# Split-weight buffers that are 256 bytes longer, with the feature-major halves written 64 bytes in

## Chip, cores and metric

The kernel runs on one core of one Trainium2 chip, as one launch. The metric is the device time of that launch in microseconds; several runs are taken and their median counts. One further execution was profiled, and every time below that is not called a median comes from it.

## What is computed

One layer of a hybrid decoder trunk over 256 tokens of width 2048, in float32. Three token mixers (gated DeltaNet, Mamba-2, GLA) share one input projection, are gated and merged, and two more sub-layers follow. Cut to what matters here:

```python
h = rmsnorm(x, pre_mix_norm[i])
... = jnp.split(h @ w_in[i], split_idx, axis=-1)          # 2048 x 15920
y_dn, y_ssm, y_gla = ...                                  # three mixers, chunked scans
up = jnp.einsum('btnm,nmd->btnd', branches, w_branch[i])  # 3 x (1024 x 2048)
mixed = jnp.sum(gates * up, axis=2) @ w_out[i]            # 2048 x 2048
x = x + rmsnorm(mixed, post_mix_norm[i])
h = rmsnorm(x, pre_mlp_norm[i])
m = jnp.square(jax.nn.relu(h @ w_up[i])) @ w_down[i]      # 2048 x 8192, 8192 x 2048
x = x + rmsnorm(m, post_mlp_norm[i])
ple_gate = jax.nn.sigmoid(rmsnorm(x, ple_pre_norm[i]) @ w_ple_gate[i])
x = x + rmsnorm((p[i] @ w_ple_proj[i]) * ple_gate, ple_post_norm[i])
```

## The kernel before

All large products run on TensorE in the type float32r. To keep float32 accuracy, each operand is split into a rounded half `hi` and the rest `lo`, and a product is three passes: hi times hi, hi times lo, lo times hi. The weights are streamed from memory and split on the way by `weights`: a 512 KB DMA on SyncE's queue brings two k-tiles of up to 512 columns into a tile `raw` (128 partitions by 2 x 512 numbers), ScalarE copies it into `hi` (line 300), and VectorE writes `raw - hi` into `lo` (line 170, the helper `tt`). Each of the three tags has four buffers of 4096 bytes per partition that are used in turn.

Two routines use the pieces. In `gemm_tok` (token-major) a 128x128 block of the activations is the stationary operand, which TensorE loads ahead of the product, and `hi` or `lo` streams through as the moving operand, 512 columns at a time (344 or 352 in some units); the profile names such a product `mm<-hi,ahi`, moving operand first. In `gemm_feat` (feature-major) a 128x128 block of `hi` or `lo` is stationary and the activations stream, 256 columns at a time: `mm<-ahi,hi`, `mm<-ahi,lo`, `mm<-alo,hi`. Both issue through line 114. Feature-major are 27 units of 192 products: 6 for DeltaNet, 3 for Mamba-2, 2 for GLA and 16 for `w_up`; all else is token-major. The order of the work on every engine is the order in which the kernel's text is written, with small pieces of the mixers (`br<-...`) put between the products by `background`.

Where the buffers lie matters for this change. In the built program all partitions have the same layout, and these are byte addresses in a partition. `hi` has its four buffers at 43360, 47456, 51552 and 55648, `lo` at 59744, 63840, 67936 and 72032; the activations `ahi` and `alo` lie at 76128 and 92512; the tiles `m` (squared MLP activations) and the split mixer outputs (profile name `b`) lie in multiples of 2048 bytes behind. All of these start at 352 modulo 512, and all operands of the large products are cut out of them at multiples of 512 bytes, except that 344 and 352 columns end earlier. So in each of the large products the stationary and the moving operand start at the same place modulo 512. A few small products of the GLA mixer do not: `gkh`, `gkl`, `ga` and the tiles with the profile name `c` start at 416 modulo 512, `gtr` at 352, `le16` (profile name `le`) at 32, and the stationary operands of the mixers' own float32 products start at many places: the first of those at 542.63 us in the rows below starts at 96 modulo 512.

Of the kernel before, what the change touches and what calls it, by code (L numbers as in the profile page):

```python
# [10 lines left out]
F32R = mybir.dt.float32r  # L11
# [4 lines left out]
P = 128  # L16
# [36 lines left out]
def tile_hybrid_block(ctx: ExitStack, tc: tile.TileContext, *args):  # L53
# [14 lines left out]
    wp = ctx.enter_context(tc.tile_pool(name="wp", bufs=4))  # L68
# [6 lines left out]
    def nm(p):  # L75
        cnt[0] += 1
        return f"{p}{cnt[0]}"
# [22 lines left out]
    def mbank(n=512):  # L100
        return ps.tile([P, n], F32, tag="mm", bufs=4, name=nm("mm_"))

    def r3(ap, b):
        return ap.rearrange("p (a b) -> p a b", b=b)
# [45 lines left out]
    def background(limit=2.6):  # L150
        end = clk[0] + limit
        go = True
        while go and clk[0] < end:
            go = False
            for t in list(tasks):
                if t.done or t.ready > clk[0] or t.blocked():
                    continue
                t.step()
                go = True
                if clk[0] >= end:  # L160
                    break
# [7 lines left out]
    def tt(eng, o, i0, i1, op):  # L169
        eng.tensor_tensor(out=o, in0=i0, in1=i1, op=op)  # L170
# [111 lines left out]
    CK = 2  # L282
# [1 line left out]

    urgent = [False]

    def weights(parts, k0, ck):

        n = sum(p[2] for p in parts)
        raw = wp.tile([P, CK, 512], F32, tag="raw", bufs=4, name=nm("raw"))[:, :ck, :]  # L290
        hi = wp.tile([P, CK, 512], F32R, tag="hi", bufs=4, name=nm("hi"))[:, :ck, :]
        lo = wp.tile([P, CK, 512], F32R, tag="lo", bufs=4, name=nm("lo"))[:, :ck, :]
        with (tc.high_priority(AHEAD) if urgent[0] else ExitStack()):
            o = 0
            for w, c, m in parts:
                nc.sync.dma_start(
                    out=raw[:, :, o:o + m],
                    in_=w[k0 * P:(k0 + ck) * P, c:c + m].rearrange("(k p) n -> p k n", p=P))
                o += m
            A.copy(out=hi[:, :, :n], in_=raw[:, :, :n])  # L300
            tt(V, lo[:, :, :n], raw[:, :, :n], hi[:, :, :n].bitcast(F32), ALU.subtract)
        return hi, lo

    def gemm_tok(parts, act, nkt, evac, k0=0, held=1):


        n = sum(p[2] for p in parts)
        pb = [mbank() for _ in range(NT)]
        steps = []
        for kc in range(0, nkt, CK):  # L310
            hl = weights(parts, k0 + kc, CK)
            steps += [(kc, k, t, hl) for k in range(CK) for t in range(NT)]
            if kc + CK == nkt:
                steps.sort(key=lambda p: p[2])
            elif kc + CK > nkt - held * CK:
                continue
            for i, (kc_, k, t, (hi, lo)) in enumerate(steps):
                kt = kc_ + k
                xh, xl = act(kt, t)
                o = pb[t][:, :n]  # L320
                PE.matmul(o, lhsT=xh, rhs=hi[:, k, :n], start=(kt == 0), stop=False)
                PE.matmul(o, lhsT=xh, rhs=lo[:, k, :n], start=False, stop=False)
                PE.matmul(o, lhsT=xl, rhs=hi[:, k, :n], start=False, stop=(kt == nkt - 1))
                if i % 2:
                    background()
                if kt == nkt - 1:
                    with tc.high_priority():
                        evac(t, pb[t][:, :n])
            steps = []

    def gemm_feat(parts, act, nkt, evac):

        n = sum(p[2] for p in parts)
        nb = n // 256
        pb = [mbank() for _ in range(nb)]
        for kc in range(0, nkt, CK):
            hi, lo = weights(parts, kc, CK)
            steps = [(k, c) for k in range(CK) for c in range(n // P)]
            if kc + CK == nkt:
                steps.sort(key=lambda p: p[1] // 2)  # L340
            for i, (k, c) in enumerate(steps):
                kt = kc + k
                xh, xl = act(kt, None)
                o = pb[c // 2][:, (c % 2) * S:(c % 2 + 1) * S]
                wh, wl = hi[:, k, c * P:(c + 1) * P], lo[:, k, c * P:(c + 1) * P]
                PE.matmul(o, lhsT=wh, rhs=xh, start=(kt == 0 and c % 2 == 0), stop=False,
                          skip_group_check=True)
                PE.matmul(o, lhsT=wl, rhs=xh, start=False, stop=False, skip_group_check=True)
                PE.matmul(o, lhsT=wh, rhs=xl, start=False, stop=(kt == nkt - 1), skip_group_check=True)
                if i % 4 == 3:  # L350
                    background()
        with tc.high_priority():
            for b in range(nb):
                evac(b, r3(pb[b], S))
# [77 lines left out]
    def feat_conv(cw, nch, ncol, c0, bias, c_w, act=hact):  # L432

        nct = ncol // P
        xp = t4()
        xp3 = r3(xp, 260)
        V.memset(xp3[:, :nct, 0:4], 0.0)

        def evac(b, pb):
            tt(V, xp3[:, 2 * b:2 * b + 2, 4:260], pb, r0bc.unsqueeze(1).broadcast_to([P, 2, S]), ALU.mult)  # L440

        gemm_feat([(w_in, c0, ncol)], act, KT, evac)
        cw, bias = cw(), bias and bias()
        y = t4()
        for c in range(nct):
            yc = y[:, c * S:(c + 1) * S]
            ch = c_w + c

            def wj(j):
                return cw[:, j * nch + ch:j * nch + ch + 1]  # L450
            if bias is None:
                A.activation(out=yc, in_=xp3[:, c, 4:260], func=AF.Copy, scale=wj(3))
            else:
                A.activation(out=yc, in_=xp3[:, c, 4:260], func=AF.Identity, scale=wj(3), bias=bias[:, ch:ch + 1])
            for j in (2, 1, 0):
                stt(yc, xp3[:, c, 1 + j:257 + j], wj(j), yc, ALU.mult, ALU.add)
        A.activation(out=y[:, :nct * S], in_=y[:, :nct * S], func=AF.Silu)
        return y
# [104 lines left out]
    def first_params():  # L563
        urgent[0] = True
        load_params()
        return prm["cw0"]
    dn_q0 = feat_conv(first_params, 24, 512, C_DNQ, None, 0, act=hact0)
    gemm_tok([(w_in, C_DNB, 352)], hact, KT, mk(0))
    dn_alog, dn_dtb, ss_alog, ss_dtb, ss_d, gainT, dcwT, scwT = (
        prm[k] for k in ("dn_alog", "dn_dtb", "ss_alog", "ss_dtb", "ss_d", "gains", "cw0", "cw1"))  # L570
# [20 lines left out]
    for c0, n in ((352, 344), (696, 344)):  # L591
        gemm_tok([(w_in, C_DNB + c0, n)], hact, KT, mk(c0))
# [174 lines left out]
    ss_dtr = const.tile([P, NT, 16], F32, name="ss_dtr")  # L767
    mk = tok_cols(16, ss_dtr, ss_y3)
    gemm_tok([(w_in, C_SDT, 16), (w_in, C_SZ, 336)], hact, KT, mk(0))
    dt = const.tile([P, NT, 16], F32, name="dt")  # L770
    adt = const.tile([P, NT, 16], F32, name="adt")
# [125 lines left out]
    def feat_plain(c0, scale):  # L897
        y = t4()

        def evac(b, pb):  # L900
            stt(r3(y[:, :1024], S)[:, 2 * b:2 * b + 2, :], pb, scale,
                r0bc.unsqueeze(1).broadcast_to([P, 2, S]), ALU.mult, ALU.mult)

        gemm_feat([(w_in, c0, 512)], hact, KT, evac)
        return y
# [101 lines left out]
    def y_tiles():  # L1007
        hi = t8().bitcast(F32R)[:, :2048]
        lo = t8().bitcast(F32R)[:, :2048]
        return r3(hi, S), r3(lo, S)  # L1010
# [21 lines left out]
    for b in range(2):  # L1032
# [8 lines left out]
        hi, lo = y_tiles()  # L1041
# [8 lines left out]
    hi, lo = y_tiles()  # L1050
# [80 lines left out]
    for cb in range(4):  # L1131
        def evac(t, pb, cb=cb):
            if cb == 0 and t == 0:
                phase_b()
            if t == 0:
                mg.append([tb("mx") for _ in range(NT)])
            if cb == 0:
                A.sqrt(out=sm(1), in_=r0[:, :1])
            square_sum(pb, 512, ssp[:, t, cb:cb + 1])
            tt(V, mg[cb][t], pb, gains["g1"][:, cb * 512:(cb + 1) * 512], ALU.mult)  # L1140
# [131 lines left out]
```

## Time and profile before

| | |
|---|---|
| median of 3 runs | 1887.17 us (1881.85 to 1887.25) |
| profiled execution, its own time | 1882.98 us |
| its span, first to last instruction | 1881.2 us |
| TensorE busy | 1846.9 us, 98% |
| VectorE busy | 1161.0 us, 62% |
| ScalarE busy | 934.9 us, 50% |
| mean granted clock of TensorE | 0.993 of full speed |
| chain that ended last | 69% of the span on TensorE, 67% on line 114 |

[...] What one product costs is the distance from its start to the start of the next one, and that is read from the timeline. [...]

### The profile page before, as it was taken

The page shows a single profiled execution, that of the slowest core. Times are in us where ns is not written, and L with a number is a line of the kernel's source. Part 1 is how long each engine was busy: PE and PEld are TensorE (multiplying, and loading weights), DVE is VectorE, ACT ScalarE, POOL GpSimd, SP SyncE. Part 2 cuts the span into 40 slices and gives each one's busy share as a digit, 9 for nine tenths or more (in the row PEclk, how much of TensorE's full clock was granted, in tenths as well). Part 3 has the DMA queues.
Part 4 walks back from the last instruction along what each step waited for, and adds up shares of the span by engine and source line. Part 5 has one row for each costly group of instructions (what it writes and reads, how often), then busy time and mean ns, then how long its engine had stood idle before and what let it go on. Part 6 is the DMA issues. An engine that isn't in the chain of part 4 may idle for free.

```text
span 1881.2 us, 28343 instructions
## 1 busy us (share of the span) xinstructions
PE 1846.9 (98%) x11256; PEld 1659.0 (88%) x11256; DVE 1161.0 (62%) x1518; ACT 934.9 (50%) x1200; POOL 183.7 (10%) x243
## 2 busy tenths in 40 slices
PE   8999999899999999999999999999999999999997
PEld 8999989899888788888888898899889988998886
DVE  6567947878566666554565755455555555555675
ACT  6745564576455564454444644444433443444664
POOL 0004814800201220000000000000000000000001
PEclk9999989999999999999999999999999999999999
DMA  7765565465665546667676565666566566656563
GB/s 250 218 184 175 147 186 165 137 182 145 196 201 168 172 143 192 195 183 196 186 246 204 175 185 190 191 189 181 191 192 188 180 192 195 184 182 195 183 207 129
DMA packets 185573, 348.07 MB, mean 185 GB/s; under 512 B 14296, under 2 KB 33103, under 8 KB 184544
## 3 DMA queue, kind: packets, MB, share of 16 engines
q1 hardware_dynamic: 182992, 334.69, 58.8%
q0 software_dynamic: 2416, 11.56, 1.8%
q8 instruction: 88, 1.44, 0.3%
q14 instruction: 45, 0.37, 0.1%
q10 hardware_dynamic: 32, 0.01, 0.0%
HBM read 340.41 MB, written 5.80 MB: 184 GB/s over the span
## 4 chain that ended last, share of the span: by engine, by line
PE 69%; ACT 1%; POOL 1%; DVE 1%; issue 0%; DMA 0%; DVEq 0%; ACTq 0%
PE mm L114 67%; PE br L114 1%; PE br L123 1%; POOL b L170 1%; DVE lo L170 0%; ACT hi L300 0%; DMA raw<-in_w_in_dram 0%; DVE b L173 0%; ACT b L946 0%; ACT L1226 0%; ACT b L945 0%; ACT b L1114 0%; ACT L1236 0%; ACT b L1224 0%; DVE s L173 0%
## 5 line engine op out<-in xcount | busy, mean ns | idle before, releaser
L170 DVE TENSOR_TENSOR lo<-raw,hi 128x1024 fp32r<-128x1024 f32 (+2 forms) x644 | 771.7, 1202 | 621.9 <-ACT hi L300 618.5
L300 ACT CAST hi<-raw 128x1024 fp32r<-128x1024 f32 (+2 forms) x644 | 653.6, 1019 | 807.3 <-PE mm L114 702.3
L114 PE MATMUL mm<-ahi,hi 128*128 128x256 f32 x1728 | 492.2, 285 | 0.0
L114 PE MATMUL mm<-ahi,lo 128*128 128x256 f32 x1728 | 490.8, 284 | 0.0
L114 PE MATMUL mm<-alo,hi 128*128 128x256 f32 x1728 | 490.8, 284 | 0.0
L114 PE MATMUL mm<-hi,ahi 128*128 128x512 f32 (+2 forms) x992 | 372.0, 375 | 0.0
L114 PE MATMUL mm<-lo,ahi 128*128 128x512 f32 (+2 forms) x992 | 369.0, 372 | 2.8 <-DVE lo L170 1.6
L114 PE MATMUL mm<-hi,alo 128*128 128x512 f32 (+2 forms) x992 | 367.6, 371 | 0.0
L114 PEld LDWEIGHTS mm<-ahi,hi 128*128 128x128 f32 x1728 | 333.3, 193 | 0.5 <-ACT ahi L180 0.2
L114 PEld LDWEIGHTS mm<-alo,hi 128*128 128x128 f32 x1728 | 332.8, 193 | 0.8 <-issue 0.8
L114 PEld LDWEIGHTS mm<-ahi,lo 128*128 128x128 f32 x1728 | 333.3, 193 | 0.1
L114 PE MATMUL mm<-hi,m 128*128 128x512 f32 x1024 | 316.0, 389 | 0.0
L114 PEld LDWEIGHTS mm<-hi,m 128*128 128x128 f32 x1024 | 192.2, 188 | 39.9
L114 PEld LDWEIGHTS mm<-lo,ahi 128*128 128x128 f32 x992 | 187.2, 189 | 32.3 <-DVE lo L170 4.0
L114 PEld LDWEIGHTS mm<-hi,ahi 128*128 128x128 f32 x992 | 187.1, 189 | 28.0 <-issue 0.2
L114 PEld LDWEIGHTS mm<-hi,alo 128*128 128x128 f32 x992 | 187.1, 189 | 27.5
L114 PE MATMUL mm<-lo,m 128*128 128x512 f32 x512 | 199.2, 389 | 0.0
L114 PE MATMUL mm<-hi,b 128*128 128x512 f32 x416 | 134.1, 393 | 0.7 <-ACT hi L300 0.7
L114 PEld LDWEIGHTS mm<-lo,m 128*128 128x128 f32 x512 | 96.1, 188 | 19.7
L170 POOL TENSOR_TENSOR b<-b 128x128 f32<-128x128 f32 (+16 forms) x118 | 78.4, 679 | 162.0 <-ACT b L939 149.9
L114 PEld LDWEIGHTS mm<-hi,b 128*128 128x128 f32 x416 | 78.1, 188 | 17.0 <-ACT hi L300 1.1
L114 PE MATMUL mm<-lo,b 128*128 128x512 f32 x208 | 81.3, 391 | 0.8 <-DVE lo L170 0.8
(257 smaller groups left out, 1130.0 us busy)
## 6 DMA issues: line engine op xcount, KB each, us to landing
raw<-in_w_in_dram SPq DMA_DIRECT2D x200, 512.0 KB, 4.1
raw<-in_w_up_dram SPq DMA_DIRECT2D x128, 512.0 KB, 3.8
raw<-in_w_down_dram SPq DMA_DIRECT2D x128, 512.0 KB, 3.8
raw<-in_w_branch_dram SPq DMA_DIRECT2D x48, 512.0 KB, 4.6
raw<-in_w_in_dram SPq DMA_DIRECT2D x48, 344.0 KB, 3.5
raw<-in_w_out_dram SPq DMA_DIRECT2D x32, 512.0 KB, 4.8
raw<-in_w_ple_gate_dram SPq DMA_DIRECT2D x32, 512.0 KB, 4.5
raw<-in_w_in_dram SPq DMA_DIRECT2D x16, 352.0 KB, 3.4
```

The lines of the kernel that those rows point to most:

```text
L114: nc.tensor.matmul(o, lhsT=lhsT, rhs=rhs, start=start, stop=stop, **kw)
L123: nc.tensor.transpose(o, i, ident)
L170: eng.tensor_tensor(out=o, in0=i0, in1=i1, op=op)
L300: A.copy(out=hi[:, :, :n], in_=raw[:, :, :n])
```

## The change

`weights` takes a new argument `off`. The buffers of `hi` and `lo` are made 64 numbers (256 bytes) longer, and the 2 x 512 numbers of a split are placed `off` numbers into the buffer: 0 where the caller is `gemm_tok`, 16 (64 bytes) where it is `gemm_feat`. `raw` is as before.

```diff
+    OFF_TOK, OFF_FEAT = 0, 16
+
-    def weights(parts, k0, ck):
+    def weights(parts, k0, ck, off):
 
         n = sum(p[2] for p in parts)
         raw = wp.tile([P, CK, 512], F32, tag="raw", bufs=4, name=nm("raw"))[:, :ck, :]
-        hi = wp.tile([P, CK, 512], F32R, tag="hi", bufs=4, name=nm("hi"))[:, :ck, :]
-        lo = wp.tile([P, CK, 512], F32R, tag="lo", bufs=4, name=nm("lo"))[:, :ck, :]
+        hi, lo = (r3(wp.tile([P, CK * 512 + 64], F32R, tag=z, bufs=4, name=nm(z))[:, off:off + CK * 512], 512)[:, :ck, :]
+                  for z in ("hi", "lo"))
...
-            hl = weights(parts, k0 + kc, CK)
+            hl = weights(parts, k0 + kc, CK, OFF_TOK)
...
-            hi, lo = weights(parts, kc, CK)
+            hi, lo = weights(parts, kc, CK, OFF_FEAT)
```

The built program has the same instructions in the same order on every engine, with the same waits; only line numbers and addresses differ. `hi` now starts at 43360, 47712, 52064 and 56416 and `lo` at 60768, 65120, 69472 and 73824, that is at 352 modulo 512 in the first and third buffer and at 96 in the second and fourth. `ahi` and `alo` move by 2048 bytes to 78176 and 94560, and so does everything behind them, which leaves their place modulo 512 as it was. In feature-major products the stationary operand therefore starts 64 bytes (first and third buffer) or 320 bytes (second and fourth) behind the moving one, modulo 512, and 64 behind modulo 256 in each of them. In token-major products the moving operand starts where the stationary one does, or 256 bytes from it.

## Rows read from the trace of the kernel before

**Rows 1.** The page, part 4: the chain that ended last, by engine.

```profile
PE 69%; ACT 1%; POOL 1%; DVE 1%; issue 0%; DMA 0%; DVEq 0%; ACTq 0%
```

**Rows 2.** Waits of TensorE: us in total, times, longest; the one for split weights.

```profile
PE mm L114 <- DVE lo L170: 2.4, 3, 0.9
```

**Rows 3.** Groups of products by form, TensorE.

```profile
line engine op names shapes xcount | busy us, mean ns | idle before us <-releasers
L114 PE MATMUL mm<-ahi,hi 128*128 128x256 f32 x1728 | 492.2, 285 | 0.0
...
L114 PE MATMUL mm<-hi,m 128*128 128x512 f32 x1024 | 316.0, 389 | 0.0
L114 PE MATMUL mm<-hi,ahi 128*128 128x512 f32 x704 | 276.5, 393 | 0.0
...
L114 PE MATMUL mm<-hi,b 128*128 128x512 f32 x416 | 134.1, 393 | 0.7 <-ACT hi L300 0.7
```

**Rows 4.** Timeline (start us, duration us, what), TensorE, feature-major, full clock.

```profile
1299.79 0.28 PE L114 MATMUL mm<-ahi,lo 128*128 128x256 f32 x1
...
1300.87 0.28 PE L114 MATMUL mm<-ahi,lo 128*128 128x256 f32 x1
```

**Rows 5.** Timeline of TensorE, token-major, 512 columns.

```profile
1199.63 0.39 PE L114 MATMUL mm<-lo,m 128*128 128x512 f32 x1
...
1200.99 0.39 PE L114 MATMUL mm<-lo,m 128*128 128x512 f32 x1
```

**Rows 6.** A stretch of 3.3 us: busy time of each engine, granted clock.

```profile
core 0: us, PE busy (x) PEld busy (x) DVE busy (x) ACT busy (x) POOL busy (x), PEclk, DMA share, GB/s
300.20:303.50 3.30, 3.30 (x16) 3.30 (x17) 3.30 (x8) 0.00 (x0) 1.27 (x2) 0.50 0.33 101
```

**Rows 7.** Timeline of TensorE in that stretch, feature-major.

```profile
302.09 0.41 PE L114 MATMUL mm<-ahi,lo 128*128 128x256 f32 x1
...
303.15 0.41 PE L114 MATMUL mm<-ahi,hi 128*128 128x256 f32 x1
```

**Rows 8.** Timeline of weight loads around the products that read le16.

```profile
504.13 0.19 PEld L114 LDWEIGHTS mm<-hi,ahi 128*128 128x128 f32 x1
...
504.81 0.19 PEld L114 LDWEIGHTS br<-le,gkh 128*128 128x128 f32 x1
505.04 0.19 PEld L114 LDWEIGHTS br<-le,gkl 128*128 128x128 f32 x1
...
505.37 0.19 PEld L114 LDWEIGHTS mm<-hi,ahi 128*128 128x128 f32 x1
```

**Rows 9.** Timeline of TensorE, the product that runs while ga is loaded.

```profile
556.92 0.39 PE L114 MATMUL mm<-hi,b 128*128 128x512 f32 x1
557.14 0.59 PE L114 MATMUL br<-b,ga 128*128 128x256 f32 x2
```

**Rows 10.** Timeline of TensorE, feature-major product while a float32 operand is loaded.

```profile
359.28 0.28 PE L114 MATMUL mm<-alo,hi 128*128 128x256 f32 x1
359.40 0.66 PE L114 MATMUL br<-c,c 128*128 128x64 f32 x5
```

**Rows 11.** Timeline of TensorE, the product of gkh that runs while gtr is loaded.

```profile
486.42 0.40 PE L114 MATMUL br<-gkh,gtr 128*128 128x512 f32 x1
486.66 0.39 PE L114 MATMUL br<-gkl,gtr 128*128 128x512 f32 x1
```

**Rows 12.** Timeline of TensorE, token-major product while weights 256 bytes apart are loaded.

```profile
542.40 0.39 PE L114 MATMUL mm<-hi,alo 128*128 128x512 f32 x1
542.63 0.49 PE L114 MATMUL br<-b,b 128*128 128x128 f32 x3
```

**Rows 13.** The page, part 5: the two instructions that write lo and hi.

```profile
L170 DVE TENSOR_TENSOR lo<-raw,hi 128x1024 fp32r<-128x1024 f32 (+2 forms) x644 | 771.7, 1202 | 621.9 <-ACT hi L300 618.5
L300 ACT CAST hi<-raw 128x1024 fp32r<-128x1024 f32 (+2 forms) x644 | 653.6, 1019 | 807.3 <-PE mm L114 702.3
```

## The prediction

> **What bounds the kernel now.** I read the chain of waits first. 69% of the span hang on TensorE, and no other engine reaches 2% [rows 1]. The waits say the same from the other side: for split weights TensorE waited 2.4 us in total [rows 2]. DMA, ScalarE and VectorE bring the weights in time, so only what changes the pace of TensorE, or makes one of those three late, can change the time.
>
> The pace is read from the timeline, as the distance between starts; the durations in the groups overlap. In the feature-major stage 9 products take 1300.87 - 1299.79 = 1.08 us, so one comes every 120 ns [rows 4]. In the token-major stage 6 products of 512 columns take 1200.99 - 1199.63 = 1.36 us, 226.7 ns each [rows 5]. The two differ by 256 columns and 106.7 ns, or 0.417 ns a column, one period of 2.4 GHz. 256 columns alone would take 106.7 ns and 512 would take 213.3: each product costs **13.3 ns more than its columns**, at either length. Where the granted clock was 0.50, the lower level of 1.2 GHz [rows 6], 5 products of 256 columns took 303.15 - 302.09 = 1.06 us, 212 ns each [rows 7], which is 256 columns at that clock with nothing over. So the 13.3 ns appear only when the moving operand streams at full rate beside the load of the next weights. The load starts with the product ahead of it: their starts, too, are 0.68 / 3 = 227 ns apart where products of 512 columns run [rows 8].
>
> The stakes follow from the counts. There are 3 x 1728 = 5184 feature-major products [rows 3], which take 5184 x 120 ns = 622 us, a third of the span. **One nanosecond per product is 5.2 us, 0.28% of the time.**
>
> **The change part by part.** *Instructions.* None is added, removed or moved, and no wait either: 0 us. Only durations can change.
>
> *Pace of the feature-major products.* This is the one large term. The change sets the stationary operand 64 bytes further in than the moving one (320 in half of the buffers); before, they agree modulo 512. Only if the 13.3 ns come from two reads that meet at places that depend on this distance can the pace move. The large products show no other distance, and yet within the same 512 bytes they show many: their operands lie at all multiples of 512 bytes from each other, and the pace is 120 ns throughout. For other distances I go to the few small products. While a `gkh` block is loaded, 64 bytes further in than the moving `hi`, just as the change has it, a product of 512 columns takes 505.04 - 504.81 = 0.23 us [rows 8], against 0.227 otherwise. While `ga` is loaded, at the same distance, it is 557.14 - 556.92 = 0.22 us [rows 9]; there are four such in the trace, all 0.22 or 0.23. A feature-major product during which a float32 operand is loaded at that distance takes 359.40 - 359.28 = 0.12 us [rows 10]. All within the 0.01 us of the view. That argues for **no change**, and I take 0 ns, since these rows have the very distance that the change makes.
>
> The bounds come from further away. Upwards: with `gtr` loaded 64 bytes short of the moving `gkh`, the product takes 486.66 - 486.42 = 0.24 us [rows 11], 0.013 more than 0.227, and its duration is 0.40 where the others have 0.39; I read +10 ns. It is a single product, and the distance has the other sign. 5184 x 10 ns = +52 us. Downwards: the weights of `le16` products, which have only 128 columns, were loaded at 505.04 and three steps later at 505.37 [rows 8], 0.33 / 3 = 0.110 us apart; I take that as the least at which loads of 128 columns follow each other. Each feature-major product needs one such load, so its pace can't fall under that: 5184 x (110 - 120) ns = -52 us.
>
> [...]
>
> *Pace of the token-major products.* Their offset is 0, yet the longer buffers put every second buffer at 96 instead of 352 modulo 512, so half of the products have a moving operand 256 bytes away from the stationary one. The count at 512 columns is 3 x 704 + 1024 + 512 + 416 + 208 = 4272 (with half as many passes over `lo` as over `hi` where `m` or `b` is stationary) [rows 3]; half is 2136. The nearest row, with weights loaded at that distance, has 542.63 - 542.40 = 0.23 us [rows 12], the same within the view's step; at most +3 ns, or 2136 x 3 ns = +6 us. Below nothing I see no reason for. I take 0.
>
> *ScalarE and VectorE.* They write the same 1024 numbers at another address. One copy takes 1.02 us and one subtraction 1.20 us on average [rows 13], each on its own engine; a group of two k-tiles feeds 24 feature-major products, 24 x 120 ns = 2.88 us, or 12 token-major ones, 2.72 us. Even if each became a third slower, TensorE would cover it. Without that cover the price would be the difference, but no row has it near. 0 us. At a pace of 110 ns the group still lasts 2.64 us, so no other engine becomes late there either.
>
> **Sum.** 1882.98 + 0 + 0 + 0 = 1883 us for the profiled execution. The three timed runs lie at 1881.85 to 1887.25, with the median at the upper end; the middle of them is 1885, and that is my number for a median of the changed kernel.
>
> **The rivals.** *The weights get out of the way.* The 13.3 ns are absent at half rate [rows 7], so they look like two reads that meet, and meetings can depend on addresses. If 64 bytes end them, the loads set the pace at 110 ns: 1885 - 52 = 1833 us; if half of the gap goes, 115 ns, it is 1859. For it speaks that `gtr` shows a distance that is not indifferent [rows 11]; against it that the same 64 bytes gain nothing in [rows 8 to 10]. Those are single products in a stream at the old distance, while the stage could settle differently when all have the new one. [...]
>
> *The weights get into the way.* If the distance acts as in [rows 11], each product costs +10 ns: 1885 + 52 = 1937 us; if only the buffers at 320 bytes are hit, half of it, 1911. It decides from 1.1 ns per product on, which is 0.3%. For it: a row that is slower at 64 bytes the other way; against it: [rows 8 to 10].
>
> *The token-major half pays.* The 256 bytes cost 3 ns in 2136 products, the rest stays: 1891 us, just slower.
>
> *The change doesn't do what it says.* The offset is there in the addresses, but modulo 512 only half of the buffers are 64 bytes on. If the distance is without effect, this is my forecast.
>
> **How the numbers follow.** About 0.3% is what a measurement here can tell from no change, 5.7 us. No effect: 0.45, with a range of its own of 1880 to 1890. Weights out of the way: 0.31, all of it faster. Weights in the way: 0.16; token-major pays: 0.08; both slower, 0.24 together. The predicted time is that of no effect, 1885. The range goes down to 1848, a pace of 112.9 ns, under which I leave a quarter of the faster case (0.08), and up to 1912, over which I leave half of the second rival (0.08).
>
> **What would show it.** In the profile after, starts of feature-major products 0.120 us apart and of token-major ones 0.227 show the forecast right; the first is where to look, in the stretches of `w_up`. A pace of 0.110 to 0.118 shows the first rival, above 0.121 the second; 0.23 and more in every second token-major group shows the third. If the weight loads, too, keep the old distance of starts, the address has no part in the 13.3 ns. The forecast is wrong if the steady pace of a whole stage depends on the distance although single products at that distance do not.

## The result, and the profile after

The changed kernel takes 1867.45 us in the median of 4 runs (1865.70 to 1870.33), the kernel before 1884.51 us in 4 runs beside it (1881.48 to 1887.25). The ratio is **0.9914, with a 95% interval of 0.9896 to 0.9931**: faster by 0.9%. The forecast was no effect, 1885 us; the range held the time, but what happened is nearest to the first rival, *the weights get out of the way*, with about a third of its full size (17 us of 52).

The profiled execution after takes 1868.37 us, its span 1866.6 us, against 1882.98 and 1881.2. First the page after: the engines, the chain that ended last, the two instructions that write the halves (they answer to [rows 1] and [rows 13]), and one form of feature-major product (busy us, mean ns of one, as in [rows 3]).

```profile
PE 1829.7 (98%) x11256; PEld 1640.7 (88%) x11256; DVE 1160.5 (62%) x1518; ACT 935.9 (50%) x1200; POOL 184.2 (10%) x243
...
PE 69%; ACT 1%; POOL 1%; DVE 1%; issue 0%; DVEq 0%; ACTq 0%
...
L170 DVE TENSOR_TENSOR lo<-raw,hi 128x1024 fp32r<-128x1024 f32 (+2 forms) x644 | 773.7, 1204 | 610.4 <-ACT hi L302 608.9
L302 ACT CAST hi<-raw 128x1024 fp32r<-128x1024 f32 (+2 forms) x644 | 654.1, 1019 | 793.2 <-PE mm L114 694.6
L114 PE MATMUL mm<-ahi,hi 128*128 128x256 f32 x1728 | 485.4, 281 | 0.0
```

The wait of TensorE for split weights, from the view of waits (us in total, times, longest; [rows 2] before):

```profile
PE mm L114 <- DVE lo L170: 2.8, 4, 0.9
```

TensorE is as full as before and waits for weights as little. It does the same 11256 operations with 17 us less of busy time (1829.7 against 1846.9), so its products come faster. How much faster is seen by counting products in a stretch of one stage that nothing interrupts. `w_up` runs as four slabs of four units each, with `w_down` between them. Below are stretches inside the four slabs: 60 us of the first, 70 us of the others; the count behind PE is that of line 114's products. First the kernel before:

```profile
core 0: us, PE busy (x) PEld busy (x), PEclk, DMA share, GB/s
1072.00:1132.00 60.00, 60.00 (x503) 60.00 (x502) 1.00 0.61 183
1240.00:1310.00 70.00, 70.00 (x586) 70.00 (x585) 1.00 0.62 185
```

and the changed kernel:

```profile
1072.00:1132.00 60.00, 60.00 (x532) 60.00 (x531) 1.00 0.66 194
1232.00:1302.00 70.00, 70.00 (x597) 70.00 (x596) 1.00 0.63 187
1410.00:1480.00 70.00, 70.00 (x597) 70.00 (x596) 1.00 0.64 188
1588.00:1658.00 70.00, 70.00 (x597) 70.00 (x596) 1.00 0.63 187
```

A count includes two or three products that reach over an edge: 70 us at 120 ns are 583, and 586 are shown. The granted clock is 1.00 in all of them. Two things are to be seen: the pace is better in every slab, and it is not one pace. The first slab gained 29 products in 60 us, the others 11 in 70 us. The timeline after (start us, duration us) gives the distances, first in the first slab, 13 products in 1121.29 - 1119.82 = 1.47 us, **113 ns** each:

```profile
1119.82 0.28 PE L114 MATMUL mm<-ahi,hi 128*128 128x256 f32 x1
...
1121.29 0.28 PE L114 MATMUL mm<-ahi,lo 128*128 128x256 f32 x1
```

then in the second slab, at the place of [rows 4], 12 products in 1301.17 - 1299.76 = 1.41 us, **117.5 ns** each:

```profile
1299.76 0.28 PE L114 MATMUL mm<-alo,hi 128*128 128x256 f32 x1
...
1301.17 0.28 PE L114 MATMUL mm<-alo,hi 128*128 128x256 f32 x1
```

and a token-major stretch, at the place of [rows 5], 6 products in 1200.31 - 1198.95 = 1.36 us, 226.7 ns each as before:

```profile
1198.95 0.39 PE L114 MATMUL mm<-lo,m 128*128 128x512 f32 x1
...
1200.31 0.39 PE L114 MATMUL mm<-lo,m 128*128 128x512 f32 x1
```

From the starts of a whole stage in the trace the two steady paces are 113.3 and 117.8 ns, and 120.0 before. Over all feature-major products (leaving out the 67 after and 77 before whose distance exceeds 130 ns, for a wait, a small product between them or the lower clock, which was 0.50 in [rows 6]), the mean is 116.36 ns after and 119.95 before. 5184 x 3.6 ns is 18.7 us; the span is shorter by 14.6. Some 2.4 us of the 4.1 between them are in the distances between token-major products, summed over the trace, but only 0.15 us of that at 512 columns; the rest of them is in the units of 344 and 352 columns, and what makes it up was not followed. The other 1.7 us lie in waits and in the changes from one kind of product to another, and were not followed either.

### The profile page after: what moved, and what is told of

Read it like the earlier page. It is cut to its first block, busy times and chain, and to the rows that moved or that the text cites. A ratio compares the mean times of both kernels' runs of the same rounds, so it can differ in the third digit from the quotient of the medians.

```text
span 1866.6 us, 28343 instructions
## 1 busy us (share of the span) xinstructions
PE 1829.7 (98%) x11256; PEld 1640.7 (88%) x11256; DVE 1160.5 (62%) x1518; ACT 935.9 (50%) x1200; POOL 184.2 (10%) x243
## 4 chain that ended last, share of the span: by engine, by line
PE 69%; ACT 1%; POOL 1%; DVE 1%; issue 0%; DVEq 0%; ACTq 0%
PE mm L114 67%; POOL b L170 1%; PE br L114 1%; PE br L123 1%; ACT hi L302 0%; DVE lo L170 0%; DVE b L173 0%; ACT b L947 0%; ACT b L948 0%; ACT L1228 0%; ACT b L1116 0%; ACT L1238 0%; ACT b L1226 0%; DVE s L173 0%; ACT b L941 0%
## 5 line engine op out<-in xcount | busy, mean ns | idle before, releaser
L170 DVE TENSOR_TENSOR lo<-raw,hi 128x1024 fp32r<-128x1024 f32 (+2 forms) x644 | 773.7, 1204 | 610.4 <-ACT hi L302 608.9
L302 ACT CAST hi<-raw 128x1024 fp32r<-128x1024 f32 (+2 forms) x644 | 654.1, 1019 | 793.2 <-PE mm L114 694.6
L114 PE MATMUL mm<-ahi,hi 128*128 128x256 f32 x1728 | 485.4, 281 | 0.0
L114 PE MATMUL mm<-alo,hi 128*128 128x256 f32 x1728 | 484.6, 281 | 0.7 <-DVE alo L173 0.7
L114 PE MATMUL mm<-ahi,lo 128*128 128x256 f32 x1728 | 484.5, 280 | 0.0
L114 PEld LDWEIGHTS mm<-ahi,lo 128*128 128x128 f32 x1728 | 329.0, 190 | 0.1
L114 PEld LDWEIGHTS mm<-alo,hi 128*128 128x128 f32 x1728 | 326.1, 189 | 1.7 <-DVE alo L173 0.9
L114 PEld LDWEIGHTS mm<-ahi,hi 128*128 128x128 f32 x1728 | 326.4, 189 | 0.6 <-ACT ahi L180 0.2
```

What stands on the lines that cost most here:

```text
L114: nc.tensor.matmul(o, lhsT=lhsT, rhs=rhs, start=start, stop=stop, **kw)
```

## The experiments

In every kernel below the products, their order and their number are the same. "Distance" is where the stationary operand starts minus where the moving one starts, modulo 256 bytes: in the changed kernel 64 in feature-major products and 0 in token-major ones. Where it is 64 modulo 512 and where it is 320, the pace is the same in the trace after: the 24 products of one buffer after the other take 113.3 ns each in the first slab, once it is steady, and 117.8 in the other three. So it is counted modulo 256 here. Diffs are against the changed kernel.

### Longer buffers alone (e1_pad_only)

```diff
-    OFF_TOK, OFF_FEAT = 0, 16
+    OFF_TOK, OFF_FEAT = 0, 0
```

> The buffers are 256 bytes longer, as in the changed kernel, but the feature-major halves start at 0 too, so stationary and moving operand agree modulo 256 again. If the distance between the two operands sets the pace: feature-major products 120 ns apart, a time within 0.3% of before. If the longer buffers or the other addresses behind them made the gain: 113 to 118 ns and a time near 1867 us.

1884.21 us in the median of 10 runs, ratio to before 0.9999 (0.9984 to 1.0014). In 70 us of `w_up`:

```profile
1242.00:1312.00 70.00, 70.00 (x585) 70.00 (x585) 1.00 0.61 182
```

The pace is that of before, 120 ns. Longer buffers and the other addresses behind them do nothing; the gain comes with the 64 bytes.

### The same offset in both operands (e2_both_64)

```diff
+    big.tile([P, 16], F32, name="shift")
     h_hi, h_lo = actpair()
```

A tile of 64 bytes that nothing uses moves the activations, and everything behind them, 64 bytes on. The halves of the weights are written exactly where the changed kernel writes them.

> The changed kernel, with the activations and all that lies behind them moved 64 bytes up as well. The weights are split to the same addresses as in the changed kernel, but the distance to the moving operand is 0 again modulo 256 in feature-major products; in token-major ones the stationary operand is now 64 bytes on. Distance theory: feature-major 120 ns, token-major at 512 columns perhaps other than 226.7 ns. Theory of the weights' own place, or of the addresses that ScalarE and VectorE write: feature-major 113 to 118 ns as in the changed kernel.

1907.35 us in one run, slower than both kernels. In 70 us of `w_up`, and in a token-major stretch of 6 products, 1401.42 - 1400.02 = 1.40 us, 233 ns each:

```profile
1256.00:1326.00 70.00, 70.00 (x585) 70.00 (x585) 1.00 0.61 183
```

```profile
1400.02 0.39 PE L114 MATMUL mm<-lo,m 128*128 128x512 f32 x1
...
1401.42 0.39 PE L114 MATMUL mm<-lo,m 128*128 128x512 f32 x1
```

Feature-major products are back at 120 ns, with the weights at the very same place. So here neither that place nor who writes there set the pace, but the distance between the stationary and the moving operand. And distance cuts both ways: token-major products, whose stationary operand now stands 64 bytes on, pay 6.6 ns each (233.3 against 226.7).

### Before's weights, the activations moved (e3_acts_192)

```diff
-    OFF_TOK, OFF_FEAT = 0, 16
+    OFF_TOK, OFF_FEAT = 0, 0
...
-        hi, lo = (r3(wp.tile([P, CK * 512 + 64], F32R, ...
+        hi, lo = (r3(wp.tile([P, CK * 512], F32R, ...
...
+    big.tile([P, 48], F32, name="shift")
     h_hi, h_lo = actpair()
```

The weight buffers are those of before; the activations move by 192 bytes, which gives feature-major products the distance 64 from the other side, and token-major ones 192.

> The kernel before with its buffers as they were, and the activations and all behind them moved by 192 bytes: the stationary operand of feature-major products is 64 bytes on modulo 256, while the weights lie and are written where they were. Distance theory: feature-major 113 to 118 ns, time about 1867 us unless the token-major products (now 64 bytes the other way) lose. Theory of the weights' own place: 120 ns, about 1884 us.

1873.86 us in one run. In the first and the second slab of `w_up`:

```profile
1075.00:1135.00 60.00, 60.00 (x512) 60.00 (x511) 1.00 0.61 185
1240.00:1310.00 70.00, 70.00 (x620) 70.00 (x620) 1.00 0.65 195
```

The distance of 64 brings the gain whichever operand is moved. The same two paces come back, but in other places: here the first slab runs at 117.8 ns and the other three at 113.3, the reverse of the changed kernel. Token-major products of 512 columns take 228.9 ns in most stages and 233.3 in the first slab of `w_down`, which takes back a part of the time.

### Other distances (e4_t16_f32, e5_sweep_up, e6_sweep_mixed)

```diff
-    OFF_TOK, OFF_FEAT = 0, 16
+    OFF_TOK, OFF_FEAT = 16, 32
```

> The offsets are 64 bytes for token-major and 128 bytes for feature-major halves. If any distance other than 0 helps: feature-major 113 to 118 ns at 128 too; if 64 is special, 120 ns or more. Token-major products have the moving operand 64 bytes on, the relation of the one slower small product of before (0.24 us): if that row tells the pace, 237 ns instead of 226.7, some 44 us more; if single products tell nothing, 226.7 ns.

1892.87 us in one run. In 70 us of `w_up`:

```profile
1245.00:1315.00 70.00, 70.00 (x593) 70.00 (x592) 1.00 0.62 187
```

At distance 128 a feature-major product takes 118.7 ns, 1.3 less than at 0; token-major ones, now with the moving operand 64 bytes on (distance 192), take 228.9 ns in most stages, but 233.3 in two of the four slabs of `w_down`. Here are 70 us in each of the first two slabs of `w_down`:

```profile
1155.00:1225.00 70.00, 70.00 (x308) 57.43 (x307) 1.00 0.61 193
1338.00:1408.00 70.00, 70.00 (x302) 56.70 (x301) 1.00 0.59 188
```

So token-major products, too, have two lasting paces at one distance. It is the distance of [rows 11], whose single product I had read as +10 ns; as a steady pace it costs 2.2 or 6.6.

Two kernels then gave each of the 16 `w_up` units an offset of its own from 0 to 240 bytes in steps of 16, and each of the 16 `w_down` units too, once in rising order and once mixed:

```diff
+        off = 4 * ((nf[0] + 5) % 16)
+        nf[0] += 1
...
-            hi, lo = weights(parts, kc, CK, OFF_FEAT)
+            hi, lo = weights(parts, kc, CK, off)
```

> Each unit has its own offset: the 16 feature-major units of the up projection get 0, 16, 32, ... 240 bytes in turn, the 16 token-major units of the down projection the same; other token-major units 0. Known so far: feature-major 120 ns at 0, 113.3 or 117.8 at 64, 118.7 at 128; token-major 226.7 at 0, 229 to 231 with the moving operand 64 bytes on, 233.3 with it 192 bytes on. If the memory is divided into pieces of 64 bytes, offsets within one piece give about the same pace (120 from 0 to 48, 113 to 118 from 64 to 112, near 118.7 from 128 to 176). [...]

> The same offsets in another order over the units, so that each is entered from another neighbour and another time in the stream. If an offset alone sets the pace, each has the pace of the run before it; if there are two paces at one offset and the entry chooses, some offsets (64 bytes above all) change between 113.3 and 117.8 ns, and offset 0 stays at 120.

1884.98 and 1881.44 us, one run each. Rows of 18 us inside one unit, of the kernel in rising order: distances 64, 112 and 224.

```profile
1236.00:1254.00 18.00, 18.00 (x161) 18.00 (x160) 1.00 0.62 186
1303.00:1321.00 18.00, 18.00 (x152) 18.00 (x151) 1.00 0.57 180
1640.00:1658.00 18.00, 18.00 (x157) 18.00 (x156) 1.00 0.68 197
```

The steady paces by distance, from the starts in the two traces (ns; two numbers where the two kernels differ):

| distance, bytes | 256 columns, feature-major | 512 columns, token-major |
|---|---|---|
| 0 | 120.0 | 226.7 |
| 16 | 118.4 | 226.7 / 236.7 |
| 32 | 118.4 | 233.3 |
| 48 | 117.8 | 234.7 / 230.0 |
| 64 | **113.3** | 233.3 |
| 80 | 118.7 | 231.1 |
| 96 | 117.3 | 234.2 |
| 112 | 120.0 | 233.3 |
| 128 | 118.7 | 233.3 / 232.3 |
| 144 | 120.0 | 231.1 |
| 160 | 120.0 | 233.3 |
| 176 | 118.1 | 231.1 |
| 192 | 117.8 | 228.9 |
| 208 | 116.7 | 233.3 |
| 224 | 116.7 | 233.3 |
| 240 | 117.3 / 120.0 | 231.7 |

The pace changes from one step of 16 bytes to the next, as between 48, 64 and 80, and not by pieces of 64 bytes; some neighbours are alike, and finer steps were not run. For products of 256 columns, 0 is among the worst and 64 the best; for 512 columns, 0 is the best and nearly all else costs 2 to 10 ns. The choice of the change, 64 for the one and 0 for the other, is the best pair that these runs show. But each pace comes from one or two stretches, in the mixers from a few more, and several distances have two: 64 (113.3 here, 117.8 in most of the changed kernel) and 240 at 256 columns; 16, 48, 128 and, with the slabs above, 192 at 512. A second pace at the others can't be excluded.

### Who decides between 113.3 and 117.8 (e8_after_again, e7_kick_208, e9_kick_0, e10_kick_48)

In the sweeps all three units at 64 bytes ran at 113.3 ns. Two of them came behind a unit at 208 bytes; the third, the first row of the rising sweep above, came behind a `w_down` unit whose offset of 48 makes a token-major distance of 208 (the expectations below speak of it as an entry from 48). In the changed kernel three slabs of four, entered from `w_down` at distance 0 or 256, ran at 117.8. So the way in might decide. First the changed kernel once more, as it is:

> The changed kernel once more, in another execution. If the pace that a stage falls into is set by the program (what stands ahead of it), the first slab runs at 113.3 and the other three at 117.8 ns as in its first profile; if it is chance, another mix. Time 1867 us, ratio to before 0.991.

1872.46 us in the median of 6 runs, ratio 0.9937 (0.9923 to 0.9952). Its first two slabs:

```profile
1074.00:1134.00 60.00, 60.00 (x512) 60.00 (x511) 1.00 0.62 188
1238.00:1308.00 70.00, 70.00 (x596) 70.00 (x596) 1.00 0.61 187
```

All four slabs run at 117.8 ns here; the first is the one that differs from the other profile of the same kernel.

Then the first weight tile of each feature-major unit (24 products) stands at 208 bytes, the rest of the unit at 64:

```diff
-            hi, lo = weights(parts, kc, CK, OFF_FEAT)
+            hi, lo = weights(parts, kc, CK, 52 if kc == 0 else OFF_FEAT)
```

> The changed kernel, but the first of the eight weight tiles of each feature-major unit lies 208 bytes in, the other seven 64. If there are two paces at 64 bytes and the way in chooses between them, and a stream that comes from 208 bytes falls into the faster one (three of three entries from another offset did in the two runs before): all units of the up projection at 113.3 ns after their first tile, a span about 10 us under that of the changed kernel, 1857 us. If the choice is chance, or set once per stage by something else: units at 117.8 as before, 1867 us.

**1858.80 us in the median of 5 runs, ratio 0.9873 (0.9856 to 0.9890)**: on the same chip 13.7 us below the unchanged change, and the shortest of all kernels here. The four slabs:

```profile
1076.00:1136.00 60.00, 60.00 (x530) 60.00 (x529) 1.00 0.63 193
1236.00:1306.00 70.00, 70.00 (x618) 70.00 (x618) 1.00 0.64 195
1410.00:1480.00 70.00, 70.00 (x618) 70.00 (x617) 1.00 0.66 194
1586.00:1656.00 70.00, 70.00 (x618) 70.00 (x617) 1.00 0.64 192
```

And the timeline where the second slab begins: 24 products at 208 bytes in 1232.06 - 1229.26 = 2.80 us, 116.7 ns each, then 36 at 64 bytes in 1236.15 - 1232.06 = 4.09 us, 113.6 ns each. The few products of the change itself cost some nanoseconds more, then 113.3 holds.

```profile
1229.26 0.28 PE L114 MATMUL mm<-ahi,hi 128*128 128x256 f32 x1
...
1232.06 0.29 PE L114 MATMUL mm<-ahi,hi 128*128 128x256 f32 x1
...
1236.15 0.28 PE L114 MATMUL mm<-ahi,hi 128*128 128x256 f32 x1
```

Is it the 208, or would any other offset ahead do? The same edit with `0` and with `12` (48 bytes) in place of `52`:

> After, but the first weight tile of each feature-major unit stands at offset 0, where its products run at 120 ns, and the rest of the unit at 64 bytes. This tells what it is in a first tile at 208 bytes that made all four w_up slabs settle at 113.3 ns. Theory A, any feature-major tile at another distance ahead does it (the direct change from a token-major product into distance 64 is what ends at 117.8): all slabs at 113.3 ns, 618 products in 70 us, about 1860 us. Theory B, only some distances do it, 208 among them: slabs at 117.8 ns, 597 products in 70 us, about 1872 us. Theory C, the choice is chance at each entry, whatever stands ahead: slabs mixed, in between. A pace that falls in this kernel to neither would show a third state.

> After, but the first weight tile of each feature-major unit stands at offset 48 bytes, where a steady unit ran at 117.8 ns, and the rest at 64. In the sweep one unit entered 64 bytes from 48 and settled at 113.3 ns. Theory A (any other feature-major distance ahead): all four slabs at 113.3 ns, 618 products in 70 us, about 1859 us. Theory B (only some distances): 113.3 ns here too if the one entry in the sweep was no chance. Theory C (chance at each entry): slabs mixed, 1860 to 1872 us. If this one and the one at offset 0 differ, B stands.

With 0 ahead: 1875.01 us in the median of 4 runs, ratio 0.9945 (0.9923 to 0.9967). All slabs run at 117.8; here are the first two:

```profile
1075.00:1135.00 60.00, 60.00 (x511) 60.00 (x510) 1.00 0.62 186
1238.00:1308.00 70.00, 70.00 (x596) 70.00 (x595) 1.00 0.62 186
```

With 48 ahead: 1872.63 us in the median of 4 runs, ratio 0.9935 (0.9910 to 0.9960). The first slab runs at 113.3, the other three at 117.8:

```profile
1070.00:1130.00 60.00, 60.00 (x530) 60.00 (x529) 1.00 0.64 194
1232.00:1302.00 70.00, 70.00 (x597) 70.00 (x596) 1.00 0.62 185
1410.00:1480.00 70.00, 70.00 (x596) 70.00 (x595) 1.00 0.62 186
1588.00:1658.00 70.00, 70.00 (x596) 70.00 (x596) 1.00 0.64 187
```

In `w_up` of e9 no unit came from 113.3, so its slabs alone can't tell whether 24 products at 0 lead to 117.8 or leave the pace as it was. One place in its mixers can, a Mamba-2 unit behind another: 9 products at 64 bytes in 304.62 - 303.60 = 1.02 us, 113.3 ns each; then 24 at 0 in 307.49 - 304.62 = 2.87 us, 119.6 each; then 36 at 64 in 311.73 - 307.49 = 4.24 us, 117.8 each.

```profile
303.60 0.28 PE L114 MATMUL mm<-ahi,hi 128*128 128x256 f32 x1
...
304.62 0.28 PE L114 MATMUL mm<-ahi,hi 128*128 128x256 f32 x1
...
307.49 0.28 PE L114 MATMUL mm<-ahi,hi 128*128 128x256 f32 x1
...
311.73 0.28 PE L114 MATMUL mm<-ahi,hi 128*128 128x256 f32 x1
```

Theory A (any other distance ahead gives 113.3) falls with the 0. Theory C (chance at each entry) falls for these entries too, since in `w_up` what was entered in one way went one way. Put together, by what ran just ahead of the products at 64 bytes, in `w_up` where nothing else is said:

| ahead of them | kernels | pace that followed |
|---|---|---|
| token-major, distance 0 or 256 | changed kernel, e8 | 117.8 in 6 slabs of 6 |
| token-major, distance 192 | e3 | 113.3 in 3 of 3 |
| feature-major, 0 | e9 | 117.8 in 15 units of 15 |
| token-major, distance 208 | e5 | 113.3 in 1 of 1 |
| feature-major, 208 | e7 | 113.3 in 15 units of 15 |
| the same | e6, one of them in the mixers | 113.3 in 2 of 2 |
| feature-major, 48, behind a unit at 64 | e10 | as the unit before: 113.3 in 3 units of the first slab, 117.8 in 9 of the others |
| feature-major, 48, behind `w_down` | e10 | 117.8 in 3 of 3 |
| small products of the mixers (first slab) | changed kernel, e7, e10 | 113.3 |
| the same | e3, e8, e9 | 117.8 |

So theory B stands in this form: some distances ahead lead to one pace or the other, 48 bytes leaves it as it was between units of `w_up`, and a steady pace lasted to the end of its slab where the products stayed at 64 bytes: 117.8 ns through the 768 products of each of the changed kernel's last three slabs. The first row's units are counted only at the start of a slab, since a pace went through unit after unit. For the same reason the weight of e7 is in its three units behind `w_down`, which without the 208 ran at 117.8, and that of e9 in the place shown above. Two things don't fit so simply. After the small products of the mixers, just ahead of which TensorE had waited (0.39 us in the changed kernel, 0.40 in e10), the same order of products led to either pace. And in the mixers of e10 a DeltaNet unit (from 84.45 us) that came from token-major products with 48 ahead went to 113.3, not to 117.8. That the changed kernel's two sets of runs differ (1865.70 to 1870.33, and 1869.55 to 1876.24) fits the profiles, one with 113.3 in the first slab and one without, but the other runs have no profile to show it.

## Where the prediction was wrong and where right, point by point

The range, 1848 to 1912 us, held the measured 1867.45, but only because the rivals had drawn it so wide. The forecast of no change and the reason given for it were wrong, so the range is no merit of the mechanism.

**What bounds the kernel: right.** TensorE is 98% busy before and after, on 69% of the chain, and the whole difference came out of its pace. **13.3 ns over the columns: the right place to look.** It is an estimate from the two paces of [rows 4] and [rows 5], 120 and 226.7 ns, as is the 2.4 GHz (1 / 0.417 ns); 1.2 GHz is half of it, at the granted clock of 0.50. 6.7 of the 13.3 ns are gone at 113.3 ns and 2.2 at 117.8. **One nanosecond per product is 5.2 us: right** as a price, less the 4 us above.

**The pace of the feature-major products: wrong.** This is the step that failed: "All within the 0.01 us of the view. That argues for no change, and I take 0 ns, since these rows have the very distance that the change makes." The readings were right, but what they were taken to show was not, for three reasons.

- *The rows were too coarse for the question.* One product read from one pair of starts is good to 10 ns, and 10 ns was the upper bound itself. The effects that the runs show are 2.2 to 6.7 ns, so the rows as printed could not have ruled them out: the 0.23 us of [rows 8] agrees with 226.7 as well as with the 233.3 ns that 512 columns take at that distance in e2. But this is not what misled. The trace holds the starts to the nanosecond, and the product of [rows 8] and the four ahead of `ga` (one is in [rows 9]) took 226 or 227 ns, that of [rows 10] 120: a finer reading would have said no change still more firmly.
- *A product of 512 columns was taken to speak for one of 256.* At 64 bytes the first gets slower (233.3 against 226.7) and the second faster (113.3 or 117.8 against 120.0).
- *Single products were taken to speak for a stage.* This is the one that decides. A single product at 64 bytes, amid others at 0, took 226 or 227 and 120 ns; whole stages at 64 take 233.3 and 113.3 or 117.8. In e3 the first three to five products at 64 bytes behind `w_down` took 116 to 124 ns before 113 was reached, and what a stage settles at depends on what ran before it. It fails in the other direction, too: the product of [rows 11] took 237 ns, where stages at its distance take 228.9 or 233.3. The prediction named this in the first rival, but gave it the smaller chance.

**The first rival: right in kind, its term too large.** The pace falls by half of the 13.3 ns at best (113.3), or a sixth (117.8), where the rival's full size was 110 ns for all 5184 products; a mean of 116.36 was measured. Its half size, 115 ns and 1859 us, is about what e7 gives, 114.0 ns and 1858.80 us. The 110 ns from the weight loads of `le16` was never reached: 113.3 is the shortest steady pace of any distance. That two reads meet was the author's reading of [rows 7]; no run shows by what the distance acts.

**Token-major: right.** The 256 bytes of every second buffer leave the pace at 226.7 to 227.0 ns; the third rival's 6 us are not there (0.15 us at 512 columns, as said above). **ScalarE and VectorE: right.** 1019 and 1204 ns against the 1019 and 1202 of [rows 13], and TensorE's wait for them is 2.8 us against 2.4. **The second rival: wrong for feature-major products.** No distance is slower than 120.0. At 512 columns a distance other than 0 does cost time, 6.6 ns at 64 bytes in e2, but the change leaves these at 0.

**The signs named in the prediction** did tell the cases apart: feature-major starts 0.113 and 0.118 us apart, within the 0.110 to 0.118 that was to show the first rival, and token-major ones still at 0.227. Its last sentence, that a whole stage could depend on the distance where single products do not, is what happened.

**What stays open:** by what the distance acts, why the same distance has two lasting paces and why 208 bytes ahead leads to one and 0 to the other, and the 4 us by which the span gained less than the feature-major products, of which only the place of 2.4 is known.

## What to carry to other kernels

Where TensorE is full and each product costs a few nanoseconds more than its columns, try the distance between the stationary and the moving operand, in steps of 16 bytes up to 256, for each length of product apart: it is one number in the code, and here it was worth 1.3% with the way into the stage included. Look at paces over hundreds of products, not at single ones: count products in long stretches of one stage, as an effect of 2 ns is far below the step of a timeline, 10 ns. Do not take a single product at a new distance, amid a stream at an old one, for what a whole stage will do.

## What was not expected of the hardware

- The pace of these float32r products depended on the distance between their two operands and changed from one step of 16 bytes to the next: 113.3 to 120.0 ns at 256 columns, 226.7 to 236.7 at 512. What was best for the one was not for the other (64 and 0 bytes). A further 256 bytes changed nothing: 113.3 or 117.8 ns at 64 and at 320, 226.7 at 0 and at 256.
- At one distance there were two steady paces, at 64 bytes and 256 columns 113.3 and 117.8 ns, at 192 bytes and 512 columns 228.9 and 233.3, each of which lasted for hundreds of products (117.8 for the 768 of a slab). At 64 bytes the products ahead decided in most places: 24 of them at 208 bytes led to 113.3 in each of the 15 units of e7, 24 at 0 to 117.8 in each of the 15 of e9, and 24 at 48 left it as it was from unit to unit in `w_up` of e10. In the first slab, behind the small products of the mixers, either came: 113.3 in the changed kernel, e7 and e10, 117.8 in e3, e8 and e9.
